# Attention of layer A: row maxima in pieces of at most 512 keys with two small buffers, and a unit's last value products ahead of the scores

## The chip, the cores and the metric

The kernel runs on one core of one Trainium2 chip. The metric is the device time of one execution in microseconds. The engines are named as in the profile: PE is the tensor engine's matmul, PEld its weight load, DVE the vector engine, ACT the scalar engine, POOL GpSimd, and SP the engine that issues the transfers (DMAs).

## The reference

A trunk of two layers for 2048 tokens of width 1024, float32. Layer A has 16 heads of width 64 with causal attention over all keys, whose logits get the cumulated logarithm of a forget gate as a bias; layer B is a windowed attention over 4 shared key heads and is not touched. The change concerns the attention of layer A:

```
q, k = rmsnorm(q), rmsnorm(k)                    # per head
c = cumsum(log_sigmoid(f_logit + b_forget))      # per head, over tokens
logits = (q @ k.T) / 8 + c[query] - c[key]
logits = where(key <= query, logits, -inf)
o = softmax(logits) @ v                          # 16 heads, 2048 x 2048
h = h + (o * silu(gate)) @ w_out
```

## The kernel before

Matmuls take float32 data rounded to a shorter form; where the accuracy matters an operand is split in a high and a low half, and the products are summed. `big`, `st`, `sq` and so on are tags of buffers in on-chip memory. `sc`, `mx`, `pa`, `pb`, `ac` and `b2` (shown as `b` in the profile) are tags of matmul accumulators in eight banks of 512 float32 columns; `BANKS_ATT` says how many buffers each has during the attention: three `sc`, one `mx` of two banks, one each of `pa`, `pb`, `ac`.

**Units and steps.** `attention_a` cuts the queries of a head into 4 chunks of 512. A unit is a head and a chunk `ch`. It has `2 * ch + 2` steps, each over two blocks of 128 keys; a head has 20 steps, the loop `for n, (u, p) in enumerate(steps)` 320. Scores are computed transposed, keys on the partitions. A step does in turn:

- `scores` (L984, L985): two matmuls a key block into two `sc` tiles, with masks on the diagonal (L989, L993); the exponential on ACT (L999, L990) into `st`; the rounded high half on ACT (L1002); the low half on POOL (L1003); the running sum of the exponentials on DVE (`ac`, L1012), and at a unit's end its sums over keys (L897).
- `values` (L1027) of the step `V_LAG` = 3 earlier: four matmuls of the low and high halves with the values into `pa`. At a unit's last step ACT copies `pa` to `sq` (L1035), and two transfers on SP bring it to memory.
- `feed`: two or three matmuls of the gate's projection (L1066, accumulator `pb`), which fill the time; every 24 of them end in a few operations on DVE and ACT (L1073 to L1075).

**Pieces of maxima.** The softmax subtracts a maximum of each row of logits. It is computed ahead, with queries on the partitions. `max_pieces` makes for each block of 128 queries `i` one or two pieces: chunks 0 and 1 have one piece of all `(i + 1) * 128` keys, chunks 2 and 3 two pieces of half as many. A piece of over 512 keys needs two matmuls, one a bank of the two-bank `mx` tile (L936). The last piece of a query block holds the diagonal; a masked maximum on DVE reads it (L947, a custom instruction, and an accumulator read behind it). The other pieces have a plain maximum (L952). Where there are two pieces, a small maximum over `mt` follows (L955). When a chunk's four query blocks are done, `to_row` sends the maxima by four transfers into a row of the queries' operand `qb`.

A head has 24 pieces. Those of the first head, `EARLY` of them, are made by a hook in the last projection group (L759), at three places in each of its last 8 token blocks, in `b2` buffers. The others are made about `AHEAD` = 13 steps ahead: `ahead(target - 1)` in front of a step's scores and `ahead(target)` behind them, with `per` = 24 pieces over 20 steps.

**Order.** A scheduler puts the instructions of each engine in an order of its own, starting from the order in which the code is written; each engine then runs its list in order and waits at semaphores. The buffers of a tag are handed on as soon as the last reader is done.

Of the kernel before, what the change touches and what calls it, by code (L numbers as in the profile page):

```python
# [14 lines left out]
BF16 = mybir.dt.bfloat16  # L15
# [4 lines left out]
AX = mybir.AxisListType  # L20
# [3 lines left out]
P = 128  # L24
# [41 lines left out]
JOBS_AT = (0, 3, 6, 9)  # L66

MAX_AT = 5
EARLY = 24
REST_AT = 3  # L70

VECTORS_AT = 8
# [16 lines left out]

BANKS = dict(b2=3, pa=1, pb=1)  # L90
BANKS_B = dict(b2=2, fl=1, pa=2, pb=1)
BANKS_ATT = dict(sc=3, mx=1, pa=1, pb=1, ac=1)


def r_(ap):
# [56 lines left out]
class Trunk:  # L152
# [696 lines left out]
    def attention_a(self, op):  # L849
# [67 lines left out]
        def max_pieces(h, ch):  # L917

            kb, qb = heads[h][1], heads[h][3]
            parts = 1 if ch < 2 else 2  # L920
            tiles = {}

            def piece(j, part):
                if "m" not in tiles:
                    tiles["m"] = self.sb("m", [P, 4], F32R, bufs=3)
                    if parts == 2:
                        tiles["mt"] = self.sb("mt", [P, 4, 2], bufs=2)
                m, mt = tiles["m"], tiles.get("mt")
                i = ch * 4 + j
                w = (i + 1) * P // parts  # L930
                k0 = part * w
                nb = 1 if w <= 512 else 2
                wb = w // nb
                ps = self.ps("mx" if "mx" in self.banks else "b2", [P, 2, 512])
                for b in range(nb):
                    mm = nc.tensor.matmul(  # L936
                        ps[:, b, :wb], qb[:66, i * P : (i + 1) * P],
                        kb[:66, k0 + b * wb : k0 + (b + 1) * wb],
                        start=True, stop=True,
                    )  # L940
# [3 lines left out]
                lg = ps[:, :nb, :wb]  # L944
                if part == parts - 1:
                    mask = mask_m[:, 1024 - w :].rearrange("p (b k) -> p b k", b=nb)
                    nc.vector.tensor_tensor_reduce(  # L947
                        out=lg, in0=lg, in1=mask, scale=1.0, scalar=NEG,
                        op0=ALU.add, op1=ALU.max, accum_out=f_(o),
                    )  # L950
                else:
                    nc.vector.reduce_max(o, lg, axis=AX.XY)  # L952
                if j == 3 and part == parts - 1:
                    if parts == 2:
                        nc.vector.reduce_max(m, mt, axis=AX.X)  # L955
# [61 lines left out]
        def values(item):  # L1017
# [14 lines left out]
            if last:  # L1032
# [4 lines left out]
                nc.sync.dma_start(out=d["om"][rows, cols], in_=ov[:HD, :])  # L1037
                nc.sync.dma_start(out=d["oc"][rows, cols], in_=ov[HD:, :])

        def gate_weights(ft, dt):  # L1040
            w = self.sb(next(weight_slots), [P, 2, 2, 2, P], F32R)
            nc.sync.dma_start(out=f_(w), in_=d["wg"][ft, :, dt // 2 : dt // 2 + 2])
            return w

        def gate():


            for ch in range(NCH):
# [6 lines left out]

                        first = gate_weights(0, 0)
                for ft in range(NDT):
                    if gate_bank == "mx":
                        ps = self.ps("mx", [P, 2, CH])[:, 0]
                    else:  # L1060
                        ps = self.ps(gate_bank, [P, CH])
# [70 lines left out]
        for n, (u, p) in enumerate(steps):  # L1132
            h, ch = units[u]
            if n % per_head == LOAD_AT and h + 1 < H:
                more_pieces(len(pieces) + 1)
            target = per * (n + AHEAD + 1) // per_head + 1
            ahead(target - 1)
            pending.append(scores(n, u, p))
            ahead(target)
            if len(pending) > V_LAG:  # L1140
                values(pending.pop(0))
            if p == 2 * ch + 1:
                if h == H - 1 and ch in (0, NCH - 1):
                    due.append((n + SUM_LAG, (h, ch and 1, ch + 1)))
                elif ch == NCH - 1:
                    due.append((n + SUM_LAG, (h,)))
            while due and due[0][0] <= n:
                recips(*due.pop(0)[1])
            feed((total - KEPT) * (n + 1) // len(steps), pause=True)
            if n == RAW_AT:  # L1150
                raw = self.sb("big", [P, NDT // 2, D])
                for p in range(NDT // 2):
                    op.weight_load(p, raw[:, p])
            if n in PREP_AT:
                op.load(PREP_AT.index(n), ("qn", "wh", "qn", "wl"))
                op.prepare(PREP_AT.index(n), nc.gpsimd)
# [348 lines left out]
    def layer_a(self):  # L1505
# [117 lines left out]
```

## Time and profile before

| | |
|---|---|
| median of 3 runs | 2460.7 us (2458.39 to 2463.78) |
| span of the profiled execution | 2459.7 us, 1.0 us below the median; its time isn't listed apart from the span |
| PE busy over the span | 2424.1 us (99%) |
| DVE, ACT, POOL busy | 1727.4 (70%), 1255.1 (51%), 1001.9 us (41%) |
| granted PE clock | 0.999 on average |
| matmuls of pieces of maxima | 660 into `mx`, 44 into `b2` |

The page counts an engine as busy while an instruction runs on it. Matmuls overlap their neighbours, so the sum over matmuls is larger than the time they take, and a busy PE can still lose time. Waits are listed as "who waits <- for whom", with the total, the number and the longest; a wait of PE for a buffer mostly shows on the weight load (PEld), which stands in front of the matmul.

### The profile page before, as it was taken

The page shows a single profiled execution, that of the slowest core. Times are in us where ns is not written, and L with a number is a line of the kernel's source. Part 1 is how long each engine was busy: PE and PEld are TensorE (multiplying, and loading weights), DVE is VectorE, ACT ScalarE, POOL GpSimd, SP SyncE. Part 2 cuts the span into 40 slices and gives each one's busy share as a digit, 9 for nine tenths or more (in the row PEclk, how much of TensorE's full clock was granted, in tenths as well). Part 3 has the DMA queues.
Part 4 walks back from the last instruction along what each step waited for, and adds up shares of the span by engine and source line. Part 5 has one row for each costly group of instructions (what it writes and reads, how often), then busy time and mean ns, then how long its engine had stood idle before and what let it go on. Part 6 is the DMA issues. An engine that isn't in the chain of part 4 may idle for free.

```text
span 2459.7 us, 36240 instructions
## 1 busy us (share of the span) xinstructions
PE 2424.1 (99%) x12016; PEld 2022.4 (82%) x12016; DVE 1727.4 (70%) x3826; ACT 1255.1 (51%) x2504; POOL 1001.9 (41%) x643
## 2 busy tenths in 40 slices
PE   8999999999999999999999999999999999999999
PEld 6788899988888887878877778888788888888887
DVE  7656567735888888888888866456766523777776
ACT  5433324323777777777777761135323312555554
POOL 0000000012877777777778862210011000377775
PEclk9999999999999999999999999999999999999999
DMA  6656545687554655465456649975434415555552
GB/s 181 207 165 193 156 145 168 192 261 223 168 155 128 210 141 150 143 198 164 133 168 182 169 137 306 290 253 153 139 90 120 137 64 165 174 176 178 180 180 73
DMA packets 351515, 419.24 MB, mean 170 GB/s; under 512 B 64928, under 2 KB 248256, under 8 KB 345152
## 3 DMA queue, kind: packets, MB, share of 16 engines
q1 hardware_dynamic: 351328, 416.92, 56.6%
q8 instruction: 95, 1.56, 0.3%
q14 instruction: 92, 0.75, 0.1%
HBM read 265.29 MB, written 151.40 MB: 169 GB/s over the span
## 4 chain that ended last, share of the span: by engine, by line
PE 46%; DVE 4%; DMA 2%; ACT 2%; POOL 2%; issue 2%; SPq 0%; DVEq 0%; ACTq 0%; POOLq 0%
PE b L759 9%; PE b L1240 5%; PE pa L1027 5%; PE pb L1453 4%; PE pb L722 3%; PE pb L1066 3%; PE b L722 3%; PE mx L936 2%; PE sc L985 2%; PE sc L984 2%; PE pa L1383 1%; PE b L1304 1%; PE pa L722 1%; PE pa L1240 1%; PE pb L1240 1%
## 5 line engine op out<-in xcount | busy, mean ns | idle before, releaser
L759 PE MATMUL b<-wh,big 128*128 128x512 f32 (+3 forms) x2560 | 770.1, 375 | 9.8 <-ACT wh L486 8.7
L1003 POOL TENSOR_TENSOR big<-st,big 128x1024 fp32r<-128x1024 f32 (+1 forms) x320 | 657.9, 2070 | 261.4 <-ACT big L1002 155.6
L759 PEld LDWEIGHTS b<-wh,big 128*128 128x128 f32 x2560 | 471.3, 188 | 81.2 <-ACT wh L486 10.5
L759 PE MATMUL b<-wl,big 128*128 128x512 f32 (+3 forms) x1280 | 474.2, 371 | 1.9 <-DVE wl L487 1.9
L1012 DVE TENSOR_TENSOR ac<-ac,st 128x512 f32<-128x512 f32 (+3 forms) x576 | 355.4, 617 | 55.6 <-ACT st L999 27.2
L999 ACT ACTIVATE st<-sc 128x512 f32<-128x512 f32 (+1 forms) x512 | 274.3, 585 | 161.8 <-PE sc L985 79.0
L1027 PE MATMUL pa<-big 128*128 128x512 f32 (+3 forms) x1280 | 326.1, 369 | 3.9 <-POOL big L1003 1.8
L1002 ACT CAST big<-st 128x1024 fp32r<-128x1024 f32 (+1 forms) x320 | 295.6, 924 | 7.8
L759 PEld LDWEIGHTS b<-wl,big 128*128 128x128 f32 x1280 | 241.4, 189 | 38.3 <-DVE wl L487 6.1
L1027 PEld LDWEIGHTS pa<-big 128*128 128x128 f32 x1280 | 222.0, 189 | 50.3 <-ACT sq L1035 17.0
L947 DVE CUSTOM_DVE_ANT_0 mx<-mx,rot 128x128 f32<-128x128 f32 (+3 forms) x240 | 210.7, 878 | 40.9 <-PE mx L936 34.8
L495 ACT ACTIVATE sq<-b,r 128x512 f32<-128x512 f32 (+2 forms) x128 | 77.8, 608 | 301.6 <-PE b L759 298.6
L984 PE MATMUL sc<-big 128*128 128x512 f32 (+3 forms) x640 | 230.1, 364 | 1.3 <-DVE st L542 1.1
L985 PE MATMUL sc<-big 67*128 67x512 f32 (+3 forms) x640 | 229.0, 367 | 0.0
L936 PE MATMUL mx<-big 66*128 66x128 f32 (+3 forms) x660 | 191.1, 363 | 3.6 <-DVE mt L947 3.1
L1066 PE MATMUL pb<-wh,wr 128*128 128x512 f32 x488 | 179.3, 398 | 2.8 <-DMA wr<-wg 2.2
L859 POOL MEMSET rot<- 128x1024 bf16 x1 | 1.0, 952 | 420.8 <-PE pb L349 420.8
L497 DVE TENSOR_REDUCE sm<-sq 128x8 f32<-128x512 f32 (+2 forms) x128 | 74.9, 585 | 138.6 <-ACT sq L495 138.4
L1352 POOL TENSOR_TENSOR big<-big,tri 128x1024 fp32r<-128x1024 f32 x60 | 143.8, 2397 | 67.1 <-DVE big L1349 62.2
L936 PEld LDWEIGHTS mx<-big 66*128 66x128 f32 x660 | 114.1, 190 | 40.9 <-DVE mt L947 11.9
L984 PEld LDWEIGHTS sc<-big 128*128 128x128 f32 x640 | 121.0, 189 | 23.1 <-DVE st L542 1.5
L985 PEld LDWEIGHTS sc<-big 67*128 67x128 f32 x640 | 121.2, 189 | 21.0
(281 smaller groups left out, 4124.8 us busy)
## 6 DMA issues: line engine op xcount, KB each, us to landing
wr<-wg SPq DMA_DIRECT2D x62, 512.0 KB
va<-st SPq DMA_DIRECT2D x32, 512.0 KB
ka<-st SPq DMA_DIRECT2D x64, 256.0 KB
ut<-big SPq DMA_DIRECT2D x16, 1024.0 KB
big<-ka SPq DMA_DIRECT2D x16, 1024.0 KB
big<-qa SPq DMA_DIRECT2D x16, 1024.0 KB
qb<-st SPq DMA_DIRECT2D x64, 256.0 KB
big<-qb SPq DMA_DIRECT2D x16, 1024.0 KB
```

Of the source, the lines that this page charges most:

```text
L722: nc.tensor.matmul(ps, W[k][dt][:, ft * P : (ft + 1) * P], u[ch][:, dt, :], start=(dt == 0 and i == 0), stop=(dt == NDT - 1 and i == 2),)
L759: nc.tensor.matmul(ps[:, :n], u[tb // 4][:, dt, us], W[k][dt], start=(dt == 0 and i == 0), stop=(dt == NDT - 1 and i == 2),)
L936: mm = nc.tensor.matmul(ps[:, b, :wb], qb[:66, i * P : (i + 1) * P], kb[:66, k0 + b * wb : k0 + (b + 1) * wb], start=True, stop=True,)
L947: nc.vector.tensor_tensor_reduce(out=lg, in0=lg, in1=mask, scale=1.0, scalar=NEG, op0=ALU.add, op1=ALU.max, accum_out=f_(o),)
L984: nc.tensor.matmul(o, ka[:, ks], qa[:, qs], start=not (last and n_), stop=False)
L985: nc.tensor.matmul(o, kb[:, ks], qb[:, qs], start=False, stop=not diag)
L999: nc.scalar.activation(pf[:, off : off + w], ps[:, :w], AF.Exp, scale=HD**-0.5)
L1002: nc.scalar.copy(ph[:, :tw], pf[:, :tw])
L1003: nc.gpsimd.tensor_tensor(pl[:, :tw], pf[:, :tw], f_(ph[:, :tw]), ALU.subtract)
L1012: nc.vector.tensor_tensor(a_, a_, pf[:, off : off + w], ALU.add)
L1027: nc.tensor.matmul(pv[:, q0 : q0 + w], v[:, k, :], src[:, off : off + w], start=(p == 0 and n_ == 0 and i == 0), stop=(last and n_ == 1 an ...
L1066: nc.tensor.matmul(ps, w[:, dt // 2 % 2, wk, dt % 2, :], us[dt][uk], start=(dt == 0 and i == 0), stop=(dt == NDT - 1 and i == 2),)
```

## The change

It does two things. First, pieces of maxima are at most 512 keys wide: a query block of chunk `ch` has `ch + 1` pieces, cut at multiples of 128 keys, so a head has 40 pieces of one matmul each. `mx` becomes two buffers of one bank in place of one buffer of two. `EARLY` becomes 40, and the hook runs at five places of a token block. Second, where the item that is due in `values` closes a unit, it is done ahead of the step's scores, with ACT's copy and the transfers behind it.

```diff
-EARLY = 24
+EARLY = 40
...
-BANKS_ATT = dict(sc=3, mx=1, pa=1, pb=1, ac=1)
+BANKS_ATT = dict(sc=3, mx=2, pa=1, pb=1, ac=1)
...
-        mask_m = self.sb("rot", [P, 1024], BF16)
+        mask_m = self.sb("rot", [P, 512], BF16)
...
-            parts = 1 if ch < 2 else 2
+            parts = ch + 1
...
-                    if parts == 2:
-                        tiles["mt"] = self.sb("mt", [P, 4, 2], bufs=2)
+                    if parts > 1:
+                        tiles["mt"] = self.sb("mt", [P, 4, NCH], bufs=2)[:, :, :parts]
...
-                w = (i + 1) * P // parts
-                k0 = part * w
-                nb = 1 if w <= 512 else 2
-                wb = w // nb
-                ps = self.ps("mx" if "mx" in self.banks else "b2", [P, 2, 512])
-                for b in range(nb):
-                    mm = nc.tensor.matmul(
-                        ps[:, b, :wb], qb[:66, i * P : (i + 1) * P],
-                        kb[:66, k0 + b * wb : k0 + (b + 1) * wb],
-                        start=True, stop=True,
-                    )
-                    if "mx" not in self.banks:
-                        self.tc.keep_in_program_order(mm)
+                k0, k1 = ((i + 1) * n // parts * P for n in (part, part + 1))
+                w = k1 - k0
+                ps = self.ps("mx" if "mx" in self.banks else "b2", [P, 512])[:, :w]
+                mm = nc.tensor.matmul(
+                    ps, qb[:66, i * P : (i + 1) * P], kb[:66, k0:k1],
+                    start=True, stop=True,
+                )
+                if "mx" not in self.banks:
+                    self.tc.keep_in_program_order(mm)
...
-                    nc.vector.reduce_max(o, lg, axis=AX.XY)
+                    nc.vector.reduce_max(o, ps, axis=AX.X)
...
+        def closes(item):
+            u, p = item[:2]
+            return p == 2 * units[u][1] + 1
...
+            ends = len(pending) == V_LAG and closes(pending[0])
+            if ends:
+                values(pending.pop(0))
             pending.append(scores(n, u, p))
             ahead(target)
-            if len(pending) > V_LAG:
+            if len(pending) > V_LAG and not ends:
                 values(pending.pop(0))
...
-            if (tb, dt) == (MAX_AT, 0) or tb >= MAX_AT + 3 and dt in (1, 4, 6):
+            if (tb, dt) == (MAX_AT, 0) or tb >= MAX_AT + 3 and dt in (0, 2, 3, 5, 6):
```

Line numbers of the changed kernel are a few lower than before: L936 becomes L933, L947 L941, L952 L946, L955 L949, L984 and L985 L978 and L979, L993 (the mask) L987, L1012 L1006, L1027 L1021, L1066 L1061.

The order of PE shows both parts. First, the two last steps of a unit before, in the middle of the attention (`mx` is a piece, `sc` the scores, `pa` the value products of three steps earlier):

```order
L936 MATMUL mx<-big 128x320 x2
L1027 MATMUL pa<-big 128x512 x4
L984 MATMUL sc<-big 128x256
L985 MATMUL sc<-big 128x256
L984 MATMUL sc<-big 128x128
L936 MATMUL mx<-big 128x384 x2
```

and now:

```order
L933 MATMUL mx<-big 128x384
L1021 MATMUL pa<-big 128x512 x4
L978 MATMUL sc<-big 128x256
L979 MATMUL sc<-big 128x256
L978 MATMUL sc<-big 128x128
L979 MATMUL sc<-big 128x128
L933 MATMUL mx<-big 128x512
```

Two pieces half a step apart were two matmuls each into the one `mx` tile, and are one matmul each into two different tiles.

Second, a unit's end on PE before, from a piece through the unit's last value products (`pa`, 256 and 128 columns) to the first ones of the next unit (512); `pb` is the gate:

```order
L936 MATMUL mx<-big 128x384
L1027 MATMUL pa<-big 128x256 x2
L1027 MATMUL pa<-big 128x128 x2
L1066 MATMUL pb<-wh,wr 128x512
L1066 MATMUL pb<-wl,wr 128x512
L984 MATMUL sc<-big 128x512
L985 MATMUL sc<-big 128x512
L984 MATMUL sc<-big 128x512
L985 MATMUL sc<-big 128x512
L936 MATMUL mx<-big 128x512
L1027 MATMUL pa<-big 128x512 x4
```

and now, from the unit's last value products on; the next unit's first ones are the sixth row after the last one shown:

```order
L1021 MATMUL pa<-big 128x256 x2
L1021 MATMUL pa<-big 128x128 x2
L978 MATMUL sc<-big 128x512
L979 MATMUL sc<-big 128x512
L978 MATMUL sc<-big 128x512
L979 MATMUL sc<-big 128x512
L933 MATMUL mx<-big 128x256
L1061 MATMUL pb<-wh,wr 128x512
L1061 MATMUL pb<-wl,wr 128x512
L933 MATMUL mx<-big 128x384
```

The last value products have moved ahead of one step's four scores, and a second step's scores now also stand between them and the next unit's products.

Third, DVE in two to three full steps before (`ac` is the running sum; an `ISA` row is the masked maximum and then its accumulator read):

```order
L947 ISA mx,mt<-mx,rot 128x2x320
L947 ISA mt 128x1
L1012 TENSOR_TENSOR ac<-ac,st 128x512
L952 TENSOR_REDUCE mt<-mx 128x1
L1012 TENSOR_TENSOR ac<-ac,st 128x512 x2
L947 ISA mx,mt<-mx,rot 128x2x352
```

and now:

```order
L941 ISA mx,mt<-mx,rot 128x512
L941 ISA mt 128x1
L1006 TENSOR_TENSOR ac<-ac,st 128x512
L946 TENSOR_REDUCE mt<-mx 128x1
L1006 TENSOR_TENSOR ac<-ac,st 128x512
L946 TENSOR_REDUCE mt<-mx 128x1
L1006 TENSOR_TENSOR ac<-ac,st 128x512
L941 ISA mx,mt<-mx,rot 128x512
```

A maximum now stands between any two additions. DVE has 272 instructions more in all, PE 64 matmuls less; ACT and POOL have as many as before. Behind the attention the order of all engines is unchanged.

More of the change, by code (lines that the diff above doesn't have):

```diff
@@ L925, in piece @@
                     tiles["m"] = self.sb("m", [P, 4], F32R, bufs=3)
[L926 to L927 removed]
+                    if parts > 1:
+                        tiles["mt"] = self.sb("mt", [P, 4, NCH], bufs=2)[:, :, :parts]
                 m, mt = tiles["m"], tiles.get("mt")
                 i = ch * 4 + j
[L930 to L942 removed]
+                k0, k1 = ((i + 1) * n // parts * P for n in (part, part + 1))
[7 more added lines that the diff above has]
+                    self.tc.keep_in_program_order(mm)
                 o = m[:, j : j + 1] if parts == 1 else mt[:, j, part : part + 1]
[L944 removed]
                 if part == parts - 1:
[L946 removed]
                     nc.vector.tensor_tensor_reduce(
[L948 removed]
+                        out=ps, in0=ps, in1=mask_m[:, 512 - w :], scale=1.0, scalar=NEG,
                         op0=ALU.add, op1=ALU.max, accum_out=f_(o),
@@ L1057, in gate @@
                 for ft in range(NDT):
[L1058 to L1061, printed above, removed]
+                    ps = self.ps(gate_bank, [P, CH])
                     for dt in range(NDT):
```

2 lines of the change are left out of this document (1 added, 1 removed).

## The prediction

> **What bounds the kernel now.** I read the page first, for the span, then the busy times of the stretch in which the attention of layer A runs and the pieces of maxima are made for the next head. The columns of a stretch are its length, then busy us of PE, PEld, DVE, ACT and POOL, with the number of instructions.
>
> ```profile
> span 2459.7 us, 36240 instructions
> ```
>
> ```profile
> 605.00:1425.00 820.00, 810.84 (x3951) 655.81 (x3950) 708.45 (x1318) 623.73 (x996) 632.16 (x312) 1.00 0.57 163
> 540.00:600.00 60.00, 58.89 (x270) 48.85 (x269) 31.12 (x55) 11.52 (x18) 1.57 (x1) 1.00 0.71 221
> ```
>
> The stretch from 605 to 1425 us is a third of the kernel. The tensor engine (PE) is busy for 810.8 of its 820 us, so it sets the pace. The vector engine (DVE) is next with 708.5, the two others have a quarter free. The stretch holds the pieces for 15 heads, hence 300 of the loop's 320 steps: 820 / 300 = 2.73 us a step. A busy PE isn't a PE at its best, since a matmul that starts late still counts from its start. What PE loses shows on its weight loads, which must wait before a matmul can. The waits of that queue in the stretch (us in all, times, longest):
>
> ```profile
> PEld pa L1027 <- ACT sq L1035: 15.9, 49, 0.6
> PEld mx L936 <- DVE mt L947: 11.9, 26, 1.0
> PEld L993 <- issue: 11.2, 65, 0.3
> PEld mx L936 <- DVE m L947: 9.3, 24, 0.5
> PEld mx L936 <- DVE mt L952: 3.7, 19, 0.4
> PEld pb L1066 <- DMA wr<-wg: 3.5, 5, 1.5
> PEld pa L1027 <- POOL big L1003: 1.6, 2, 1.0
> PEld pb L1066 <- DVE sq L1075: 1.3, 2, 0.7
> PEld sc L984 <- ACT st L999: 1.2, 3, 0.6
> ```
>
> Two causes stand out. Three rows say that a piece of maxima (`mx`) waits until DVE has read the piece before it: 11.9 + 9.3 + 3.7 = 24.9 us, 69 times. One row says that the first value product of a unit (`pa`) waits until ACT has copied the unit before out of the only `pa` bank: 15.9 us, 49 times. Together 40.8 us, 1.7% of the kernel. These two are what the change touches. The other side of the first one stands in DVE's own waits:
>
> ```profile
> DVE mx L947 <- PE mx L936: 34.8, 67, 1.4
> DVE mt L952 <- PE mx L936: 25.4, 58, 0.8
> ```
>
> DVE waits 60.2 us for pieces and PE waits 24.9 us for DVE: with one `mx` buffer they take turns. The next rows are the timeline of DVE, then of PEld, over one such turn (start, duration):
>
> ```profile
> 700.13 1.03 DVE L947 CUSTOM_DVE_ANT_0 mx<-mx,rot 128x832 f32<-128x832 f32 x1
> ...
> 701.99 1.09 DVE L952 TENSOR_REDUCE mt<-mx 128x1 f32<-128x896 f32 x1 [0.30 <-PE mx L936]
> ...
> 704.16 1.10 DVE L947 CUSTOM_DVE_ANT_0 mx<-mx,rot 128x896 f32<-128x896 f32 x1
> 705.18 0.14 DVE L947 DVE_READ_ACCUMULATOR2_ANT mt<- 128x1 f32 x1
> ```
>
> ```profile
> 701.28 0.30 PEld L936 LDWEIGHTS mx<-big 66*128 66x128 f32 x2 [0.61 <-DVE mt L947]
> ...
> 703.32 0.43 PEld L936 LDWEIGHTS mx<-big 66*128 66x128 f32 x2
> ```
>
> The piece at 701.28 had to wait 0.61 us for the maximum that began at 700.13. From its weight load to the end of its own maximum (701.99 + 1.09 = 703.08) it took 1.80 us; the next, from 703.32 to 705.26, took 1.94 us. So a piece occupies its buffer for 1.8 to 1.9 us. A piece half a step behind another (1.4 us) is late, a piece a whole step behind (2.73 us) is not.
>
> **The change part by part.** *Two small tiles for one of two banks.* There are now 40 pieces a head and not 24, so two in each step: one ahead of the scores, one behind them. Each goes to the tile that the piece before the last had, and that piece stood a full step earlier. By the turnaround above 2.73 us are enough for 1.9. The reductions are also shorter. I take away 21 of the 24.9 us and leave 4 for places where the order puts two pieces side by side or DVE is behind; the ends are 0 and 24.9.
>
> *Same columns on PE.* The widths of a head's pieces sum to 17408 columns before and after; 44 matmuls a head become 40. At best 64 weight loads of 0.19 us less are 12 us, but those loads run beside matmuls (PEld has 655.8 of 820 us busy, PE 810.8), so I take 0.
>
> *More and smaller vector instructions.* Masked maxima: 16 a head as before, none now wider than 512 (one of 128, one of 256, four of 384, ten of 512). Plain maxima: 24 a head and not 8 (one of 256, 13 of 384, ten of 512). Small maxima of the `mt` columns: 3 and not 2. The groups of the stretch, then the shapes (busy us, mean ns):
>
> ```profile
> L947 DVE CUSTOM_DVE_ANT_0 mx<-mx,rot 128x128 f32<-128x128 f32 (+3 forms) x239 | 209.5, 877 | 40.9 <-PE mx L936 34.8 <-DMA om<-sq 0.7 <-DMA big<-m 0.3
> L952 DVE TENSOR_REDUCE mt<-mx 128x1 f32<-128x576 f32 (+3 forms) x120 | 118.4, 986 | 26.2 <-PE mx L936 25.4
> ```
>
> ```profile
> L952 DVE TENSOR_REDUCE mt<-mx 128x1 f32<-128x1024 f32 x15 | 18.1, 1208 | 0.0
> ...
> L952 DVE TENSOR_REDUCE mt<-mx 128x1 f32<-128x576 f32 x15 | 11.3, 751 | 1.6 <-PE mx L936 1.5
> L947 DVE CUSTOM_DVE_ANT_0 mx<-mx,rot 128x512 f32<-128x512 f32 x15 | 10.4, 696 | 1.6 <-PE mx L936 1.6
> L947 DVE CUSTOM_DVE_ANT_0 mx<-mx,rot 128x384 f32<-128x384 f32 x15 | 8.4, 559 | 0.8 <-PE mx L936 0.7
> L947 DVE CUSTOM_DVE_ANT_0 mx<-mx,rot 128x256 f32<-128x256 f32 x15 | 6.4, 424 | 2.7 <-PE mx L936 2.6
> L955 DVE TENSOR_REDUCE m<-mt 128x4 fp32r<-128x8 f32 x29 | 4.4, 150 | 0.2
> L947 DVE CUSTOM_DVE_ANT_0 mx<-mx,rot 128x128 f32<-128x128 f32 x15 | 4.3, 290 | 0.2 <-PE mx L936 0.2
> ```
>
> Before, a head's masked maxima are 16 x 877 ns = 14.0 us and the plain ones 8 x 986 = 7.9. After, the masked ones are 0.29 + 0.42 + 4 x 0.56 + 10 x 0.70 = 9.9 us. Plain maxima of 384 and 512 don't occur before; along the line from 576 (751 ns) to 1024 (1208 ns), 1.02 ns a column, they are 555 and 686 ns, and 256 is 425: 0.43 + 13 x 0.555 + 10 x 0.686 = 14.5 us. With one `m` maximum more (0.15): 24.6 - 21.9 = 2.7 us a head, 40 us over 15 heads, on DVE. That is the upper end. In the rows above the accumulator read starts at 705.18 while the maximum ahead of it lasts until 705.26, so an instruction hides 0.08 us of itself under its neighbour; 17 more a head give back 17 x 0.08 x 15 = 20 us. So DVE gets 20 to 40 us more work, into 820 - 708.5 = 111.5 us of idle time, 60 of which are the waits for pieces that go. If that cover is gone, the running sums on DVE (`ac`) come later, then the exponentials on ACT, then the score tiles that PE needs. Price on PE: 0 if DVE always catches up; at 40 us see the first rival, 19 us. I take 9, the middle.
>
> The Trainium skill, "VectorE: DVE Perf Modes", section "The DRAIN you can't avoid", says that the next vector instruction does not start until the pipe has emptied, and its rules ask to keep the number of instructions small. By that rule the added work is the full 40 us and the sum below ends at 2444, not 2434; the 0.08 us of overlap in the rows speaks against the strict form of it.
>
> *The unit's end ahead of the scores.* The timeline of PE, ACT and POOL at one unit's end before:
>
> ```profile
> 734.69 0.39 PE L984 MATMUL sc<-big 128*128 128x512 f32 x1
> ...
> 735.88 0.57 PE L1027 MATMUL pa<-big 128*128 128x256 f32 x4
> ...
> 738.63 1.20 PE L1027 MATMUL pa<-big 128*128 128x512 f32 x4 [0.35 <-ACT sq L1035]
> ```
>
> ```profile
> 738.01 0.56 ACT L1035 COPY sq<-pa 128x512 f32<-128x512 f32 x1
> ```
>
> ```profile
> 727.05 3.08 POOL L1003 TENSOR_TENSOR big<-st,big 128x896 fp32r<-128x896 f32 x2 [0.20 <-PE mx L936]
> ```
>
> The last value products (735.88) stand behind the four scores that start at 734.69, and the copy runs from 738.01 to 738.57, behind ACT work of the same step; the next unit's first product waits 0.35 us for it. Moved ahead of the scores, the last products start about 1.2 us earlier and the copy stands ahead of that step's exponentials, while the next unit's first product stays a step later. That is 1.2 us plus two exponentials earlier against 0.6 us of longest wait, so I take away 14 of 15.9 us; the ends are 0 and 15.9. What is behind the copy: that step's exponentials start 0.56 us later. There are three score tiles, and a wait of the scores for exponentials is 1.2 us in all now; that cost is in the 9 us. On SP the two transfers of the copied unit are issued behind the copy, earlier in the program than before; nobody on PE waits for them, and the number of transfers is the same (the row of each block of maxima still leaves as four).
>
> *The first head's pieces.* They run beside the last projection group, five a block of tokens and not three, in the three `b` buffers that the block's own sums use. PE loses next to nothing there (58.9 of 60 us busy, of which the start of the attention takes most of the rest), and DVE is half free (31.1 of 60), so 2.7 us more of maxima are hidden. If a piece must wait for a buffer, it is at most one maximum of 0.7 us in each of 8 blocks, 6 us; I take 1. The mask is half as wide and is made once, on a POOL that is idle there: 0.
>
> Sum against the profiled execution, whose span is 2459.7 us, 1.0 us under the median of 2460.7: 2459.7 - 21 - 14 + 9 + 1 = 2434.7, rounded down to 2434 for the 64 weight loads.
>
> **The rivals.** *The vector engine becomes the bound.* Its 708.5 us plus 40 plus the 51 us of idle time that isn't waiting for pieces (111.5 - 60.2) is 799.9: the stretch gets shorter by 20 us, not 34, and the time is about 2440. For it: DVE would be 94% busy. Against: at the 20 us end the same sum is 780, below what PE needs.
>
> *Everything goes.* All 40.8 us of waits vanish and DVE's extra work stays hidden: 2459.7 - 40.8 = 2419. Against it: PE at 99% and DVE at 86% wait for each other 85 us now, and DVE gets fuller.
>
> *The waits only move.* PE waits for score tiles or for POOL in place of maxima and copies, since ACT, POOL and DVE all feed it, and the time stays at 2460. For it: an in-order chain of four engines. Against: the waits of scores and values for ACT and POOL are 1.2 and 1.6 us now.
>
> *The last products come too early* (slower). They read the low halves that POOL makes, and are moved ahead by four scores. If POOL were the latest there, each of some 60 unit ends would wait for up to the 0.93 us that four scores take: 56 us, so 2459.7 - 35 + 10 + 56 = 2491. It decides from 25 / 60 = 0.42 us a unit's end. Against: the POOL row above ends at 730.13, and the products that need it start at 735.88, 5.7 us later; only 2 waits of that kind are in the list.
>
> **How the numbers follow.** My forecast of 2434 has 0.53. The vector engine as the bound (2440) has 0.20, everything goes (2419) 0.10, the waits move (2460) 0.11, too early (2491) 0.06. About 0.2% (5 us) is what a measurement of this kernel can tell from no change; faster by more holds the first three, 0.83; the same is 0.10, slower 0.07. The range runs from 2417 (all waits gone, with 2 us for the weight loads) to 2453, part of the way to the case without a gain; it leaves out the last two.
>
> **What the changed profile would show.** PEld's waits of `mx` for DVE should fall from 24.9 us to under 8, and those of `pa` for ACT's copy from 15.9 to under 4. DVE's busy time in the attention should rise by 20 to 40 us in a stretch some 25 us shorter, and its waits for `mx` fall below 30. Plain maxima of 512 columns should last about 0.69 us. The prediction is wrong if new rows of `sc` on ACT, or `pa` on POOL, take more than 15 us together, if a piece of 512 columns costs DVE as much as one of 1024, or if the last projection group loses more than 6 us.

## The result and the profile after

The changed kernel takes 2440.38 us (median of 4 runs, 2438.39 to 2441.85) against 2461.93 us (4 runs, 2458.39 to 2463.78) for the kernel before in the same comparison: a ratio of 0.9915, 95% interval 0.9902 to 0.9929, or 21.6 us less. Against the later runs of the kernel before (2460.31 to 2461.14 us, given with the experiments) it is 20 to 21 us. The forecast was 2434 in a range of 2417 to 2453. The profiled executions differ by 19.6 us, 17.7 of them between the first and the last value product of layer A's attention (from 861.0 us to 843.3, start to start). The head of the page after (busy us, share of the span, instructions):

```profile
span 2440.1 us, 36268 instructions
...
PE 2408.3 (99%) x11952; PEld 2025.6 (83%) x11952; DVE 1728.7 (71%) x4098; ACT 1258.6 (52%) x2504; POOL 998.5 (41%) x643
```

The same two stretches as in the prediction (length, then busy us of PE, PEld, DVE, ACT and POOL with their instructions). The first is 15 us shorter since the attention now runs through it faster:

```profile
605.00:1410.00 805.00, 797.82 (x3903) 660.46 (x3901) 708.35 (x1577) 629.41 (x999) 631.47 (x313) 1.00 0.58 168
540.00:600.00 60.00, 59.90 (x270) 49.25 (x269) 33.08 (x70) 10.62 (x17) 0.68 (x1) 1.00 0.70 213
```

DVE has 1577 instructions there in place of 1318, and is busy for 708.35 us in place of 708.45. PE is still the busiest engine. The waits of PE's weight loads in that stretch (us in all, times, longest):

```profile
PEld L987 <- issue: 9.8, 60, 0.2
PEld pb L1061 <- DMA wr<-wg: 9.0, 7, 4.4
PEld sc L906 <- issue: 2.6, 11, 0.2
PEld mx L933 <- DVE m L941: 2.2, 8, 0.3
PEld mx L933 <- DVE mt L941: 1.5, 6, 0.4
PEld mx L933 <- DVE mt L946: 1.5, 6, 0.3
PEld pa L1021 <- POOL big L997: 1.0, 2, 0.8
PEld pa L1021 <- ACT sq L1029: 0.5, 2, 0.3
```

Both waits that the change aimed at are nearly gone: pieces of maxima wait 2.2 + 1.5 + 1.5 = 5.2 us for DVE in place of 24.9, and value products wait 0.5 us for ACT's copy in place of 15.9. In this stretch the waits of the scores for ACT (0.3 us) and of the values for POOL (1.0) haven't grown. New are short waits of a sum at a head's end that also uses an `sc` tile (L906), 2.6 us for no cause that the profile names and 0.9 for ACT. What has grown most is the wait of the gate's matmuls for their weights, 9.0 us in place of 3.5. DVE's own waits for pieces:

```profile
DVE mt L946 <- PE mx L933: 28.3, 65, 1.0
...
DVE mx L941 <- PE mx L933: 18.4, 21, 2.7
```

That is 46.7 us in place of 60.2. The two groups of maxima, and the plain ones of 512 columns alone (busy us, mean ns, idle before):

```profile
L946 DVE TENSOR_REDUCE mt<-mx 128x1 f32<-128x384 f32 (+1 forms) x360 | 213.9, 597 | 30.5 <-PE mx L933 28.3
L941 DVE CUSTOM_DVE_ANT_0 mx<-mx,rot 128x384 f32<-128x384 f32 (+2 forms) x240 | 146.8, 616 | 19.4 <-PE mx L933 18.4
```

```profile
L946 DVE TENSOR_REDUCE mt<-mx 128x1 f32<-128x512 f32 x150 | 101.7, 678 | 14.6 <-PE mx L933 13.0
```

The listed waits fell by 19.7 + 15.4 = 35.1 us and the weights' rose by 5.5, which leaves 29.6; the span fell by 19.6. The forecast too had a gap, of 10 us between the 35 us of waits and the 25 of its gain, and filled it with 9 us of price for vector work. Two questions follow. Is it vector work that takes the rest back? And what is a listed microsecond of waiting worth? In the expectations below, reading A is that PE's two waits are what the change took away and vector work is hidden; reading B is that DVE has become the bound, the first rival of the prediction, whose time (2440) the result happens to meet.

### The profile page after: what moved, and what is told of

Read it like the earlier page. It is cut to its first block, busy times and chain, and to the rows that moved or that the text cites. A ratio compares the mean times of both kernels' runs of the same rounds, so it can differ in the third digit from the quotient of the medians.

```text
span 2440.1 us, 36268 instructions
## 1 busy us (share of the span) xinstructions
PE 2408.3 (99%) x11952; PEld 2025.6 (83%) x11952; DVE 1728.7 (71%) x4098; ACT 1258.6 (52%) x2504; POOL 998.5 (41%) x643
## 4 chain that ended last, share of the span: by engine, by line
PE 86%; DVE 4%; DMA 4%; ACT 2%; issue 1%; POOL 1%; SPq 1%; ACTq 0%; DVEq 0%; POOLq 0%
PE b L759 27%; PE pa L1021 10%; PE pb L1061 7%; PE b L1238 5%; PE sc L979 5%; PE sc L978 5%; PE pb L1451 5%; PE mx L933 5%; PE pb L722 3%; PE b L722 3%; PE pa L1381 2%; PE b L1302 2%; DMA wr<-wg 1%; PE pa L349 1%; PE pb L349 1%
## 5 line engine op out<-in xcount | busy, mean ns | idle before, releaser
L759 PEld LDWEIGHTS b<-wh,big 128*128 128x128 f32 x2560 | 472.3, 189 | 81.3 <-ACT wh L486 10.7
L1006 DVE TENSOR_TENSOR ac<-ac,st 128x512 f32<-128x512 f32 (+3 forms) x576 | 352.3, 612 | 55.1 <-ACT st L993 29.3
L993 ACT ACTIVATE st<-sc 128x512 f32<-128x512 f32 (+1 forms) x512 | 273.1, 582 | 127.5 <-PE sc L979 59.5
L1021 PE MATMUL pa<-big 128*128 128x512 f32 (+3 forms) x1280 | 318.7, 365 | 1.0 <-POOL big L997 1.0
L1021 PEld LDWEIGHTS pa<-big 128*128 128x128 f32 x1280 | 229.5, 190 | 40.4 <-POOL big L997 3.0
L946 DVE TENSOR_REDUCE mt<-mx 128x1 f32<-128x384 f32 (+1 forms) x360 | 213.9, 597 | 30.5 <-PE mx L933 28.3
L978 PE MATMUL sc<-big 128*128 128x512 f32 (+3 forms) x640 | 232.8, 368 | 0.1
L979 PE MATMUL sc<-big 67*128 67x512 f32 (+3 forms) x640 | 229.4, 367 | 0.0
L933 PE MATMUL mx<-big 66*128 66x512 f32 (+2 forms) x600 | 224.6, 379 | 0.2
L1061 PE MATMUL pb<-wh,wr 128*128 128x512 f32 x488 | 178.8, 399 | 6.7 <-DMA wr<-wg 6.7
L941 DVE CUSTOM_DVE_ANT_0 mx<-mx,rot 128x384 f32<-128x384 f32 (+2 forms) x240 | 146.8, 616 | 19.4 <-PE mx L933 18.4
L978 PEld LDWEIGHTS sc<-big 128*128 128x128 f32 x640 | 121.9, 190 | 21.6 <-DVE st L542 0.5
L979 PEld LDWEIGHTS sc<-big 67*128 67x128 f32 x640 | 122.1, 191 | 19.4
```

The source lines that it names most:

```text
L759: nc.tensor.matmul(ps[:, :n], u[tb // 4][:, dt, us], W[k][dt], start=(dt == 0 and i == 0), stop=(dt == NDT - 1 and i == 2),)
L933: mm = nc.tensor.matmul(ps, qb[:66, i * P : (i + 1) * P], kb[:66, k0:k1], start=True, stop=True,)
L941: nc.vector.tensor_tensor_reduce(out=ps, in0=ps, in1=mask_m[:, 512 - w :], scale=1.0, scalar=NEG, op0=ALU.add, op1=ALU.max, accum_out=f_(o),)
L946: nc.vector.reduce_max(o, ps, axis=AX.X)
L978: nc.tensor.matmul(o, ka[:, ks], qa[:, qs], start=not (last and n_), stop=False)
L979: nc.tensor.matmul(o, kb[:, ks], qb[:, qs], start=False, stop=not diag)
```

## The experiments

All times stand beside runs of the kernel before on the same chip, which gave 2460.55 us for the first four kernels, 2461.14 for the next four, 2460.45 for the three after and 2460.31 for the last. A difference between two experiments is taken after each has been set against its own runs of the kernel before (2461.93 us for the changed kernel), unless it is said to be one of medians.

### The pieces alone, and the unit's end alone

The changed kernel with the old order at a unit's end:

```diff
-            ends = len(pending) == V_LAG and closes(pending[0])
+            ends = False
```

> The changed kernel with the last value products left behind the scores: pieces and two small tiles alone. Theory A (two separate waits of PE were removed, and what is missing of the gain is lost elsewhere, mostly to late gate weights): the waits of mx for DVE stay near 5 us, those of pa for the copy come back at 14 to 18 us, time 2448 to 2455. Theory B (the vector engine has become the bound, so that the time no longer depends on the copy): 2438 to 2444, as the changed kernel.

The kernel before with the new order at a unit's end alone:

```diff
+        def closes(item):
+            u, p = item[:2]
+            return p == 2 * units[u][1] + 1
...
+            ends = len(pending) == V_LAG and closes(pending[0])
+            if ends:
+                values(pending.pop(0))
             pending.append(scores(n, u, p))
             ahead(target)
-            if len(pending) > V_LAG:
+            if len(pending) > V_LAG and not ends:
```

> The kernel before with only the last value products and the copy moved ahead of the scores. Theory A: waits of pa for the copy under 2 us, waits of mx for DVE near 25 us as before, time 2445 to 2451, so that this gain and that of the pieces alone sum to the 21 us of both. Theory B: the vector engine has no more work than before, so the whole 15 us show and more than the sum: 2444 to 2447, and the two parts together would then be worth less than their sum by 8 us or more.

The pieces alone took 2456.57 us (ratio 0.9984, 0.9975 to 0.9993), 4.0 less than before; the unit's end alone 2453.81 (0.9972, 0.9962 to 0.9981), 6.7 less. Both are slower than reading A expected, and far from reading B. Together that is 10.7 us, half of the 21.6 that both bring, where reading A had expected the whole. Weight-load waits of the pieces alone, then of the unit's end alone:

```profile
PEld pa L1021 <- ACT sq L1029: 21.2, 54, 1.0
...
PEld pb L1061 <- DMA wr<-wg: 10.0, 7, 1.8
PEld mx L933 <- DVE mt L941: 1.8, 7, 0.3
PEld mx L933 <- DVE m L941: 1.6, 6, 0.3
PEld mx L933 <- DVE mt L946: 1.2, 6, 0.3
```

```profile
PEld mx L936 <- DVE mt L947: 18.4, 49, 0.9
...
PEld pb L1070 <- DMA wr<-wg: 9.2, 7, 2.4
PEld mx L936 <- DVE m L947: 7.9, 26, 0.5
...
PEld mx L936 <- DVE mt L952: 2.9, 16, 0.3
```

Each part takes its own wait away, and the other wait grows: the copy's from 15.9 to 21.2 us, the maxima's from 24.9 to 29.2. Probably a PE that isn't held at one place arrives earlier at the other; that isn't shown, since the order on PE differs too. Each also pays for the weights, 10.0 and 9.2 us in place of 3.5. So the parts are worth less singly than together: the growth of the other wait (5.3 and 4.3 us) falls away when both are done, and the weights are paid once and not twice (7 us). At the price worked out below these 16 us are 11 to 12, about the difference between 21.6 and 10.7.

### One tile in place of two

The changed kernel, small pieces and all, with a single one-bank buffer:

```diff
-BANKS_ATT = dict(sc=3, mx=2, pa=1, pb=1, ac=1)
+BANKS_ATT = dict(sc=3, mx=1, pa=1, pb=1, ac=1)
```

> The changed kernel with one mx tile of one bank and not two (a bank stays unused). Theory A: a piece half a step behind another must wait for its reading; with 600 pieces about half wait 0.2 to 0.4 us, so 60 to 120 us of waits of mx for DVE and a time of 2490 to 2550. A rival (the smaller pieces are what helped, since each is read sooner): waits under 25 us, time 2440 to 2455.

2475.40 us, a ratio of 1.0060 (1.0047 to 1.0074): slower than before by 14.9 us, 36.4 us slower than with two tiles. That lies between the two cases that were expected.

```profile
PEld mx L933 <- DVE mt L946: 24.3, 110, 1.1
PEld mx L933 <- DVE mt L941: 22.5, 78, 0.7
...
PEld mx L933 <- DVE m L941: 6.9, 27, 0.5
```

Without the second tile the small pieces wait 53.7 us, 215 times. So the smaller piece alone doesn't take the waits away, and the second tile does; the smaller piece makes room for it in the same two banks. Two tiles of two banks each don't fit beside the others in eight banks and were not tried.

### Less and more work on the vector engine

First the changed kernel with 192 of the running sums of 512 columns left out (the denominators of the softmax are then too small), and the sums bounded below by an added instruction:

```diff
             nc.vector.tensor_tensor(rc, ps, roots[:nr, 1 if c0 else 0], ALU.mult)
+            nc.vector.tensor_single_scalar(rc, rc, 1e-3, ALU.max)
             nc.vector.reciprocal(rc, rc)
...
-                if p == 0 and n_ == 0:
+                if p == 0 and n_ == 0 or not diag and n_ == 1:
                     continue
```

> The changed kernel with 192 of the running sum's additions of 512 columns left out (the second key block of each full step; the sums are then bounded from below by one small instruction a head), which takes some 135 us of vector work out of the attention. Theory A (DVE is not the bound): 2434 to 2441, at most the 5 us of mx waits and a little of ACT. Theory B (DVE is the bound): 2425 or below.

2464.39 us (ratio 1.0013, 1.0004 to 1.0022): 25 us slower than the changed kernel, with less work. The added instruction stands behind it, as the last experiment shows, which differs in that instruction alone. A row of the weight loads' waits, then one of DVE, then one of POOL:

```profile
PEld mx L934 <- DVE mt L947: 18.4, 12, 1.8
```

```profile
1370.19 2.08 DVE L912 TENSOR_SCALAR sq<-sq 64x32 f32<-64x32 f32 x1
```

```profile
1370.12 2.12 POOL L998 TENSOR_TENSOR big<-st,big 128x896 fp32r<-128x896 f32 x1 [0.27 <-ACT big L997]
```

An instruction on 64 x 32 numbers lasted up to 2.08 us (1.71 on average over 14, the shortest 0.63), in the rows above until POOL's instruction ended (1372.24 and 1372.27 us); in 12 cases a piece of maxima waited some 1.5 us for DVE behind it. Hence this run told nothing on reading B. The last experiment repeated it with the bound inside an instruction that is there already:

```diff
-            nc.vector.tensor_tensor(rc, ps, roots[:nr, 1 if c0 else 0], ALU.mult)
+            nc.vector.scalar_tensor_tensor(rc, ps, 1e-3, roots[:nr, 1 if c0 else 0], ALU.max, ALU.mult)
```

> The changed kernel with the same 192 running sums of 512 columns left out (about 0.6 us each, 115 us of the vector engine's work), so the softmax's denominators are too small. The bound on the sums now stands inside an instruction that is there already, so the extra instruction of the first try (14 times up to 2.08 us in its trace, with some 1.5 us of waits for maxima behind each) is gone. Theory A (what came back isn't vector work; PE waits little for the vector engine): 2436 to 2441, with waits of pieces for the vector engine at 2 to 5 us. Rival B (the vector engine's added work is what costs the 6 us by which the result lies over the forecast, or more): 2426 to 2433. If the time is over 2445 the order of the instructions has changed for the worse again and the run tells nothing.

2440.46 us (ratio 0.9917, 0.9903 to 0.9931). The other way round, the changed kernel with the first plain maximum of each query block of the last chunk made twice:

```diff
                     nc.vector.reduce_max(o, ps, axis=AX.X)
+                    if ch == NCH - 1 and part == 0:
+                        nc.vector.reduce_max(o, ps, axis=AX.X)
```

> The changed kernel with the first plain maximum of each query block of the last chunk done twice: 60 instructions of 0.56 to 0.69 us, 36 us more vector work, as much as the change itself added by its row durations. Theory A (the vector engine still has room): 2438 to 2448. Theory B (it is the bound): 2465 to 2476.

2441.66 us (0.9918, 0.9903 to 0.9933). The attention's stretch with less, then with more vector work:

```profile
605.00:1410.00 805.00, 795.82 (x3896) 660.15 (x3894) 620.05 (x1395) 627.70 (x996) 630.41 (x312) 1.00 0.58 167
```

```profile
605.00:1410.00 805.00, 799.74 (x3919) 661.24 (x3918) 734.08 (x1641) 634.84 (x1002) 634.36 (x313) 1.00 0.58 167
```

DVE was busy for 620, 708 and 734 us of 805, and the kernel took 2440.46, 2440.38 and 2441.66. Over a span of 114 us of vector work the median moves by about 1 us. The listed weight waits moved against it (11.7, 9.0 and 7.8 us), which at the price worked out below could hide 3 us, still far from 9 us for a third of that work; and the attention of the profiled executions got no longer with more vector work (844.3, 843.3 and 839.9 us, from the first to the last value product). Reading B is refuted; so is a price of 9 us for vector work.

### The gate's weights

The longest weight wait after the change, on PE (start, duration; in the rows that follow `wg` are the weights, `ut` the operands of a new chunk, `big<-m` the row of maxima):

```profile
1054.60 0.67 PE L1061 MATMUL pb<-wh,wr 128*128 128x512 f32 x1 [4.09 <-DMA wr<-wg]
```

The same place in the kernel before, on PE and on SP:

```profile
1063.79 0.50 PE L1066 MATMUL pb<-wh,wr 128*128 128x512 f32 x1 [1.24 <-DMA wr<-wg]
```

```profile
1057.96 0.38 SPq L1042 DMA_DIRECT2D wr<-wg  x1
```

And SP after the change:

```profile
1032.16 8.30 SPq L560 DMA_DIRECT2D big<-m  x8
...
1041.84 0.54 SPq L1051 DMA_DIRECT2D wh<-ut  x1
...
1046.14 0.60 SPq L1040 DMA_DIRECT2D wr<-wg  x1
1048.13 3.02 SPq L560 DMA_DIRECT2D big<-m  x4
1051.20 0.59 SPq L1051 DMA_DIRECT2D wh<-ut  x1
```

When the gate begins a new chunk of tokens, its first weights are issued at 1046.14, behind eight transfers of rows of maxima (some 0.5 to 0.6 us each; the 8.30 us of that row hold a wait of 3.4) and behind six of the sixteen operand loads. Before the change they stand behind six operand loads too. PE has reached the gate's matmul some 4 us after that issue in both kernels (at 1050.2 and 1062.3); but from the issue to the matmul it took 8.5 us after the change and 5.8 before. So at this place, half of the listed 9.0 us, the transfer took longer to be there; PE didn't come earlier. Why it took longer isn't shown: four rows of maxima and three operand loads follow it on SP before PE goes on, where before there were one and six.

The expectations name 15.7 us of weight waits, and 5.7 before. These add the list of the weight loads (9.0 and 3.5) to that of the matmuls (6.7 and 2.2), which show the same waits twice. Three kernels bear on the weights, all the changed kernel otherwise. The weights ahead of the operands:

```diff
-                rows, us, first = self.factor_rows(0, ch), [], None
+                rows, us = self.factor_rows(0, ch), []
+                first = gate_weights(0, 0)
...
-                    if dt == NDT // 2 - 1:
-
-                        first = gate_weights(0, 0)
```

> The changed kernel with the first gate weights of a gate chunk asked for ahead of that chunk's operands and not after half of them. Theory A (PE's waits for gate weights, 15.7 us where the kernel before had 5.7, come at the chunk's start, where the weights queue behind the operands): these waits fall by 4 to 6 us and the time to 2434 to 2437. Theory C (they come because PE reaches the gate's matmuls earlier than any transfer can be there, since the transfer can only start when a buffer comes free): nothing changes, 2438 to 2443.

A new chunk's loads three steps ahead of its first matmul, which is caught up later:

```diff
+                if ch:
+                    yield
                 for ft in range(NDT):
...
+            if pause:
+                n = min(n, fed + 5)
...
+                if fed % (3 * NDT * NDT) == 0:
+                    next(filler, None)
+                    rest = 3
+                    if pause:
+                        break
...
```

> The changed kernel with the loads of a new gate chunk issued three steps ahead of its first matmul, and at most five gate matmuls caught up in one step. Theory A: the waits for gate weights fall from 15.7 us to under 6, time 2429 to 2434. Theory C: the waits at the chunk starts go but those inside chunks stay or grow, 2435 to 2441.

And the gate's weights loaded once into each buffer and used for all its matmuls, which leaves out 62 of the 64 transfers of 512 KB (the expectation counts 60) and makes the gate another one:

```diff
+        kept = {}
...
-            w = self.sb(next(weight_slots), [P, 2, 2, 2, P], F32R)
+            slot = next(weight_slots)
+            if slot in kept:
+                return kept[slot]
+            kept[slot] = w = self.sb(slot, [P, 2, 2, 2, P], F32R)
```

> The changed kernel that loads gate weights once and uses them for every gate matmul of the attention, which leaves out 60 transfers of 512 KB (the gate is then wrong). It shows what all waits for gate weights cost. Theory A: the waits are 0 and the time falls by the 15 us that they make up, to 2422 to 2428. Theory B (something else sets the pace, and PE would only wait elsewhere): 2435 to 2441.

Later both edits of the loads were put in one kernel:

> The changed kernel with both edits to the gate's loads: a new chunk's first weights asked for ahead of its operands, and the chunk's loads three steps earlier. Weights first alone gave 2437.1 (5.0 us of weight waits left), loads earlier alone 2440.5 (6.1 us left); all weight waits away gave 2432.8. If the two work on different stalls, the waits fall to 1 to 3 us and the time to 2434 to 2436; if they work on the same ones or the catching up of matmuls costs what the loads save, 2437 to 2441.

The listed weight waits of the weights first, the loads ahead, and both:

```profile
PEld pb L1059 <- DMA wr<-wg: 5.0, 5, 1.9
```

```profile
PEld pb L1063 <- DMA wr<-wg: 6.1, 5, 2.2
```

```profile
PEld pb L1061 <- DMA wr<-wg: 2.8, 4, 1.8
```

Times: 2437.08 us for the weights first (ratio 0.9899, 0.9884 to 0.9914), 2440.48 for the loads ahead (0.9913, 0.9898 to 0.9928), 2437.16 for both (0.9903, 0.9889 to 0.9918), 2432.77 without the loads (0.9883, 0.9866 to 0.9899). The weights first did about what theory A said: the long wait is gone, and 4.0 of the 9.0 us with it. The loads ahead gained nothing, alone or on top of the other: what they save is lost again, probably in the gate's matmuls that must be caught up (not shown). The kernel without loads lies between its two cases. The weights first is the fastest version that leaves nothing out; its lead of 2.5 to 3.3 us over the changed kernel is hardly more than can be told apart, as the two intervals overlap. Without any weight loads the kernel lies 6.8 us further below its kernel before than the changed one does (28.4 against 21.6), and comes to 2433, where the forecast stood. That experiment also takes the traffic of the loads away, so it bounds the weights' share from above.

### The copy made twice

The copy out of `pa` doubled, once in the kernel with the pieces alone (the copy late), once in the changed kernel (the copy early):

```diff
                 nc.scalar.copy(ov, pv)
+                nc.scalar.copy(ov, pv)
```

> The pieces alone (unit's end behind the scores) with ACT's copy of the unit out of `pa` made twice, 0.56 us more behind each of 64 units' ends, 50 of them in the attention's pieces stretch. The pieces alone took 2456.6 us and showed 22.3 us of `pa` waits for the copy on the weight loads' list, 56 times. The waits get about 0.56 us longer each: the list should show some 50 to 58 us. Theory S (the weight loads' wait counts less a fixed 0.2 us each, since the matmul ahead still runs; what is added to a wait that is there already counts in full): 2456.6 + 31 to 36 = 2488 to 2492. Rival T (a listed wait is worth a constant share of about 0.65, the rest is made up later): 2456.6 + 20 to 23 = 2477 to 2480. Rival U (a listed wait costs nothing in the end, the order makes it up): under 2465.

> The changed kernel with the same copy made twice, where it stands ahead of the step's exponentials. The prediction said that the copy has 1.2 us and two exponentials of lead there against a longest wait of 0.6 us. If that lead is real, a copy 0.56 us longer still lies in it: `pa` waits for the copy stay below 3 us, the exponentials come 0.56 us later behind three score tiles, and the time is 2440 to 2446. Rival: the lead was just enough for one copy, or the scores now wait for exponentials: waits of 0.2 to 0.5 us at 50 to 64 ends, 2452 to 2470.

Late: 2468.04 us (1.0030, 1.0014 to 1.0047), 11.6 us more than the pieces alone, and none of the three cases. ACT around a unit's end in that kernel, then two rows of its weight-load waits:

```profile
740.03 0.59 ACT L1029 COPY sq<-pa 128x512 f32<-128x512 f32 x1
740.51 0.62 ACT L993 ACTIVATE st<-sc 128x512 f32<-128x512 f32 x1
741.00 0.60 ACT L1030 COPY sq<-pa 128x512 f32<-128x512 f32 x1
```

```profile
PEld pa L1021 <- ACT sq L1030: 21.3, 47, 0.8
PEld pb L1062 <- DMA wr<-wg: 13.3, 8, 2.5
```

The copies take 1.57 us there, with an exponential between them, and yet the wait is listed at 21.3 us as with one copy. At this place five more gate matmuls and one more piece stand on PE ahead of the next unit's first products than with one copy. So the order changed with the edit, and the run doesn't measure what a longer wait costs.

Early: 2448.12 us (0.9946, 0.9929 to 0.9962), 9.2 us more than with one copy (7.7 by the medians), over the upper end of 2446 and under the rival's 2452. Its waits:

```profile
PEld mx L933 <- DVE mt L946: 3.3, 13, 0.5
PEld sc L978 <- ACT st L993: 2.8, 13, 0.4
...
PEld pa L1021 <- ACT sq L1030: 1.8, 7, 0.4
```

The value products wait 1.8 us for the longer copy, 0.5 with one, so the lead that the prediction worked out is real, for all but a few ends. The scores now wait a little for exponentials, which stand behind the copy, and the pieces 2.4 us more for DVE. No single row accounts for the 9.2 us.

## Why the prediction was right, and where not

**The maxima's waits (21 of 24.9 us taken away).** They fell by 19.7 to 5.2, under the 8 named. The one-tile kernel shows that it takes the second tile.

**The copy's waits (14 of 15.9).** They fell by 15.4 to 0.5, under the 4 named. Moved ahead, the copy has lead for most of a second one.

**The price of vector work (9 us): the step that failed.** "Price on PE: 0 if DVE always catches up; at 40 us see the first rival, 19 us. I take 9, the middle." It is about 0: from 620 to 734 us of DVE's work the median stays within about 1 us. Already its input was wrong. The durations of the maxima rose by 213.9 + 146.8 - 209.5 - 118.4 = 32.8 us, near the 40 forecast, but DVE's busy time, forecast to rise by 20 to 40, fell by 0.1: neighbours overlap more. The prediction counted 17 more overlaps a head, of 0.08 us; the rows of the trace hold 27 more of that size. The forecast that its waits for pieces fall below 30 us missed too (46.7): a DVE that keeps up goes on waiting for PE. So most of the idle time that was to cover the added work, and was thought to go, stayed.

**A listed wait taken as time lost (implicit in the 21 and the 14).** This step was too large, and its excess had nearly the size of the price above, with the other sign. The row of the prediction at 738.63 shows it: PE's matmul is 0.35 us late, and the weight load in front of it is listed with 0.61 us, since the matmul ahead was still running when that load could have begun:

```profile
738.62 0.77 PEld L1027 LDWEIGHTS pa<-big 128*128 128x128 f32 x4 [0.61 <-ACT sq L1035]
```

The list of PE's own waits before the change, which the prediction didn't use, is far shorter:

```profile
PE mx L936 <- DVE mt L947: 3.1, 15, 0.7
PE pb L1066 <- DMA wr<-wg: 2.2, 4, 1.2
...
PE pa L1027 <- ACT sq L1035: 0.7, 2, 0.4
```

So the loss to maxima and copies lies somewhere between 3.8 and 40.8 us. The undone parts price it. Against the changed kernel, the unit's end alone lists 29.2 - 5.2 = 24.0 us more of waits for maxima and is 21.6 - 6.7 = 14.8 us slower (0.62); the pieces alone list 20.7 us more for the copy and are 17.6 us slower (0.85); one tile lists 48.5 more and is 36.4 slower (0.75). Each of these differences is uncertain by 3 to 5 us, and other rows move a little too, but three times it is 0.6 to 0.85 us per listed microsecond, some 0.75. The attention of the profiled executions (first to last value product) gives a little less: it is 12.4, 14.9 and 34.7 us longer, hence 0.52, 0.72 and 0.72, some 0.65. With that, the 35.1 us that went are worth 23 to 26. The list isn't always too long. In the first kernel with less vector work the waits for maxima last 1.5 us each, not 0.25 to 0.4 as in the three; from 598 to 1450 us its maxima list 18.0 us more than the changed kernel's and its weights 4.3, and its attention is 22.2 us longer: each listed microsecond counts.

**What came back: the weights.** The prediction had no term for them. They list 5.5 us more; taking all 9.0 away was worth 6.8 by medians and 9.9 in the profiled attention, traffic included, so the rise costs 4 to 6. By medians that is 26 less 4, or 22, beside the measured 21.6; in the profiled attention 23 less 6, or 17, beside 17.7. The share comes from this same kernel with parts undone, so the sum shows that the account closes, not that it holds elsewhere. Why the weights are waited for longer with each variant (7.8 to 13.3 us in all but those that change the loads, against 3.5 before) isn't settled. At the longest wait it is the time from issue to use that grew, 5.8 to 8.5 us, and not PE's lead.

**The smaller terms.** The first head's 40 pieces cost nothing that shows: the first value product starts at 599.6 us, at 599.4 before. Plain maxima of 512 columns take 0.678 us, forecast 0.686.

**The rivals.** The vector engine as the bound is refuted, although its time was the nearest. "Everything goes" would have been 2419. The waits did move in one place, from one of the two parts to the other when only one is done, which the rival didn't say; with both done only the weights' grew. The last products aren't too early: `pa` waits 1.0 us for POOL in the stretch (over the whole loop, from 598 to 1450 us, 3.0 in place of 1.6). That the forecast missed by only 6 us thus rests on two correct mechanisms and on luck: waits that counted 9 to 12 us too much and a price of 9 us that isn't there cancel, and most of what is left is the weights' term that it lacked.

## What to carry to other kernels

Don't take a wait listed on PE's weight loads for time lost: here short ones, of 0.25 to 0.4 us on average, were worth some half to 0.85 of what was listed, and long ones, of over a microsecond, about all of it. For the short ones the matmuls' own list showed far less than was lost. Price a wait by undoing one part, and don't explain the difference by the engine that happens to be next in busy time, before more and less work has been tried on it. Two short waits on the same in-order engine can replace each other, as here, so it is worth trying them together; a test of each alone undersold both. Splitting work so that its buffer becomes two of half the size paid through the second buffer: the same split with one buffer was slower than no split.

## What the runs showed of the hardware

259 more vector instructions in the attention's stretch, 32.8 us more of maxima in summed durations, left DVE's busy time where it was (708.45 and 708.35 us); the sums of the other large group, `ac`, moved by 2.4 us only. So more work ran under a neighbour. Counted in the rows of the trace, 860 of 1318 vector instructions began before the one ahead had ended, and 1268 of 1577 after the change, both by 0.085 us in the median; the overlap in all rose from 82 to 117 us. The Trainium skill, "VectorE: DVE Perf Modes", section "The DRAIN you can't avoid", has the next instruction wait until the pipe is empty; it adds that an instruction that isn't held starts earlier, and it is this addition that the traces agree with. Which instructions were held the rows don't say.

A vector instruction on 64 x 32 numbers with a constant took between 0.63 and 2.08 us; the reciprocal of the same 64 x 32 numbers takes 0.33. All 15 of these started while POOL was at work, and each ended 0.03 to 0.04 us after the POOL instruction that had started before it. Where POOL was idle the same instruction, on 16 and on 48 partitions, took 0.17 us each time, as in this row:

```profile
1432.01 0.17 DVE L912 TENSOR_SCALAR sq<-sq 16x32 f32<-16x32 f32 x1
```

The Trainium skill, "SBUF — State Buffer", section "Who interferes with whom", says that such an operation can need ports shared with GpSimd, and that whoever starts first keeps them for the whole instruction. These ends agree with it. The one plain alternative, that such an instruction is slow by itself, doesn't fit the 0.17 us.
